# One hybrid attention layer on one core: gated-linear-attention scores and states joined, the first FoX scores begun with the third tile, and low parts put in fixed places

## The chip, the core and the metric

The kernel runs on one core of one Trainium2 chip. The metric is the device time of one execution in microseconds (us). The engines are named as in the profile: PE (TensorE, the matrix multiplier, with PEld for its weight loads), DVE (VectorE), ACT (ScalarE), POOL (GpSimd) and SP (SyncE, which issues most DMAs here). Each works through its own list of instructions in order, and waits on semaphores of the others.

## What is computed

One layer on 512 frames of width 1024 (`D`), after an RMSNorm. One wide projection feeds three branches; each is gated by a sigmoid, the sum goes through `w_out`, and an MLP with squared ReLU follows. Cut to what the change touches:

```python
# FoX branch: 8 heads of 64, causal softmax with a decay F
s = einsum('bhqd,bhkd->bhqk', q, k) * scale + F_q - F_k
p = softmax(where(k_pos <= q_pos, s, -inf)); out = p @ v
# GLA branch: 4 heads, dk 64, dv 128, chunks of 64 frames
a_causal = (q * exp(b)) @ (k * exp(-b)).T
a_anti   = (q * exp(-b)) @ (k * exp(b)).T
attn     = where(lower, a_causal, a_anti)
o = attn @ v + (q * exp(b)) @ state        # state carried from chunk to chunk, decayed
# third branch: cross attention into 256 memory tokens
merged = gate0 * y_gla + gate1 * y_fox + gate2 * y_mem
h = h + merged @ w_out;  h = h + relu(rms(h) @ w_ff1)**2 @ w_ff2
```

## The kernel before

**Numbers in two parts.** A float32 operand of a large product is split into a high part (a cast by ACT, names ending in `h` or `hi`) and a low part (source minus high part, a subtraction by DVE, names ending in `l` or `lo`). `mm3` (lines 154 to 157) then makes three matmuls of each product: high by high, low by high, high by low. Weights go through three rotating buffers: `load_w` loads one chunk, `split_w` (142) splits it; the cast is line 145, the low part line 146.

**Order of work.** PE's list stands exactly as the program is written. The other engines' lists are made by a scheduler; `tc.issue_after(x)` keeps instructions behind `x` in it. `weave` (192) runs a list of steps, and between them as many units of filler as the steps' shares ask for; a unit is one k-step of a projection, three 512-column matmuls. PSUM is cut into two pools of four banks: `mmt` (85, tiles called `mm`) and `at_` (88, tiles called `a`). A tile of a pool can be written only when the last reader of the bank's former tile is done.

**FoX.** The heads go in pairs. `fox_pair(j)` projects queries and keys; their low parts `Ql` (488) and `Kl` (492) are kept in the list `pend` and written when `low_parts()` is called. `fox_scores(j)` makes the score tiles of both heads, tile i holding 128 queries by 128(i+1) keys: tiles 0 and 1 lie in two `mmt` banks, tiles 2 and 3 in four `at_` banks (537). Then follow mask, maximum, exponential (549) and the scaling by the reciprocal sum (551). `fox_turn(h)` transposes the probabilities by PE and splits them into `PTh` (ACT) and `PTl` (DVE, 209), and then calls `low_parts`; `fox_values(h)` multiplies by V (574, 575). Ahead of the first pair's scores PE makes the V projection, whose four `mmt` banks are emptied by line 209 (`V`), and four passes of `mem_rows` (386) into an `at_` bank that ACT empties in line 387.

**GLA.** Two pairs of heads. `decays(j)` makes the decay factors (755 on PE) and the four scaled operands; `key_turn(j)` transposes keys (781); `gla_scores(j, m)` makes the causal (m=0) or mirrored (m=1) scores, a matmul over 64 rows for each head (815), and copies the wanted half into `at` with eight predicated copies (818); `states(j)` makes chunk states (794; 800 and 801 on DVE); `gla_values(j)` puts both together (826, 830); `gla_turn(h)` transposes the result (847) and multiplies it by `sg` (849). Lines 876 to 881 give the steps and shares; the filler is the projections of `gla_g` and `fox_late`.

**Gates.** `gate_group` makes the gate projections by a seven-product scheme. In its first group `lefts_2` (926) makes new left operands from `u`: `xsum[1]` gets one block subtracted (928) and one added (929), then comes the cast (930) and the low part (931). The second call makes `f2h` and `f2l`, which the matmuls of block 22 read (product 3). `take(6, ...)` adds product 6 to sums called `ct` in operations of line 957.

Of the kernel before, what the change touches and what calls it, by code (L numbers as in the profile page):

```python
# [9 lines left out]
F32 = mybir.dt.float32  # L10
# [4 lines left out]
ALU = mybir.AluOpType  # L15
AX = mybir.AxisListType

P = 128
# [4 lines left out]
NT = S // P  # L23
# [41 lines left out]
def hybrid_block(ctx, tc, chunks, wst, memT, xN, cols, gffn, gfin, wup, cst, out):  # L65
    nc = tc.nc
# [5 lines left out]
    def nm(s):  # L72
        uid[0] += 1
        return f"{s}_{uid[0]}"
# [22 lines left out]
    msk_s = cp.tile([P, 2, P], U8, name="msk_s")  # L97
# [44 lines left out]
    def split_w(raw):  # L142
        hi = wp.tile([P, 1024], F32R, tag="hi", name=nm("whi"))
        lo = wp.tile([P, 1024], F32R, tag="lo", name=nm("wlo"))
        cast = nc.scalar.copy(hi, raw)  # L145
        low_now[0] = nc.vector.tensor_tensor(lo, raw, f(hi), op=ALU.subtract).ins  # L146
        cast_now[0] = cast.ins
        next_sum(cast.ins)
        return hi, lo
# [251 lines left out]
    with pool("fox") as xp:  # L401
# [121 lines left out]
        def fox_scores(j):  # L523

            qh, ql, kh, kl = QK[j]
            stat = [[xp.tile([P, NT], F32, tag=f"{g}{e}", name=nm(g)) for g in ("mx", "rs", "ri")] for e in range(2)]
            live.update({2 * j + e: [] for e in range(2)})
            low = [mmt() for _ in range(2)]
            banks = {}
            for i in range(NT):  # L530
                n = P * (i + 1)
                w = max(n, 256)
                ps = [x[:, 256 * i:256 * i + 256] for x in low] if i < 2 else [at_()[:, :n] for _ in range(2)]
                sl = slice(i * P, (i + 1) * P)
                for p, (q, k) in enumerate(((qh, kh), (qh, kl), (ql, kh))):
                    for e, a in enumerate(half):
                        nc.tensor.matmul(ps[e], q[a, sl], k[a, :w], start=p == 0, stop=p == 2)  # L537
                banks[i] = ps
            for e in range(2):
                nFb = rows[2 * j + e]  # L540
                for i in range(NT):
                    n = P * (i + 1)
                    r = (nFb[:, 7:8, :], nFb[:, 0:2, :], nFb[:, 0:7:3, :], nFb[:, 2:6, :])[i]
                    mx, rs, ri = (x[:, i:i + 1] for x in stat[e])
                    Pt = xp.tile([P, n], F32, tag=f"Pt{i}", name=nm("Pt"), bufs=2)
                    by = [x.rearrange("p (b t) -> p b t", t=P) for x in (Pt, banks[i][e][:, :n])]
                    nc.vector.tensor_tensor_reduce(out=by[0], in0=by[1], in1=r, scale=-1.0, scalar=3e38,
                                                   op0=ALU.add, op1=ALU.min, accum_out=mx)
                    nc.scalar.activation(Pt, Pt, AF.Exp, bias=mx, scale=-1.0, accum_out=rs)
                    nc.vector.reciprocal(ri, rs)  # L550
                    nc.vector.tensor_scalar(Pt, Pt, ri, None, op0=ALU.mult)
                    live[2 * j + e].append(Pt)

        def fox_turn(h):
            Ps = live.pop(h)
# [60 lines left out]
        with tc.issue_after(cast_now[0]):  # L616
            mem_split()
        run(pair)
        low_parts()

        gvg = v_chunks(OFF["gv"], lambda t, ps: nc.scalar.copy(gv[:, t, :], ps))
        T, V_, R, A = fox_turn, fox_values, fox_rows, fox_scores
# [125 lines left out]
    with pool("gla") as lp:  # L748
# [36 lines left out]
        def states(j):  # L785


            dec, kt = gs["d", j][0], gs["k", j]
            mid = gs["s", j] = lp.tile([P, NT, P], F32, tag="mid", name=nm("mid"))
            pv = at_([P, NT, P])  # L790
            for t in range(NT - 1):
                for e in range(2):
                    h = 2 * j + e
                    nc.tensor.matmul(pv[64 * e:64 * e + 64, t, :], kt[:, t, 64 * e:64 * e + 64], gv[:, t, h * P:(h + 1) * P],
                                     start=True, stop=True)
            for t in range(NT - 1):
# [4 lines left out]
                nc.vector.tensor_scalar(mid[:, t + 1, :], x, dec[:, t:t + 1], None, op0=ALU.mult)  # L801

        def gla_scores(j, m):

            _, kn, kp, qp, qn = gs["d", j]
            kk, qq = ((kn, qp), (kp, qn))[m]
            if m == 0:
                gs["a", j] = [lp.tile([P, NT, P], F32, tag=f"at{e}", name=nm("at")) for e in range(2)]
                for at in gs["a", j]:
                    nc.gpsimd.memset(at, 0.0)  # L810
            ps = [at_([P, NT, P]) for _ in range(2)]
            for t in range(NT):
                sl = slice(t * P, (t + 1) * P)
                for e in range(2):
                    nc.tensor.matmul(ps[e][:, t, :], kk[half[e], sl], qq[half[e], sl], start=True, stop=True)  # L815
            for e in range(2):
                for t in range(NT):
                    nc.vector.copy_predicated(gs["a", j][e][:, t, :], msk_s[:, m, :], ps[e][:, t, :])

        def gla_values(j):  # L820
            mid, qp = gs["s", j], gs["d", j][3]
# [48 lines left out]
        def gate_ready(b):  # L870
# [36 lines left out]
    with pool("outp") as op_:  # L907
# [18 lines left out]
        def lefts_2(to, block):  # L926
            with tc.issue_after(low_now[0]):
                nc.vector.tensor_tensor(xsum[1], block[0], xsum[1], op=ALU.subtract)
                nc.vector.tensor_tensor(xsum[1], xsum[1], block[1], op=ALU.add)
                cast = nc.scalar.copy(to[0], xsum[1]).ins  # L930
                nc.vector.tensor_tensor(to[1], xsum[1], f(to[0]), op=ALU.subtract)
            return cast

        loaded, summed = [None], [None]

        def gate_group(gate, wo, oh, ol, i, ready=None, last=None):
# [25 lines left out]
            def product(n, w):  # L962
                wh, wl = (t.rearrange("p (a k c) -> p a k c", a=2, k=4) for t in w)
                uh, ul = GATE[n]
                ps = mmt([P, 2, 256])
                for a in range(2):
                    for k in range(4):
                        mm3(ps[:, a, :], wh[:, a, k, :], wl[:, a, k, :], uh[:, k, :], ul[:, k, :], k == 0, k == 3)
                return ps

            def take(n, ps):
                if n == 1:
                    nc.scalar.copy(c21, ps)
                if n == 2:
                    vec(c11, c21, ps)
                    tanh(c11)
                if n == 5:
                    nc.scalar.copy(c22, ps)
                if n == 6:
                    vec(c21, c21, ps, ALU.subtract)  # L980
                    vec(c22, c22, c21, ALU.subtract)
                if n == 3:
                    vec(c12, c22, ps)
                    tanh(c12)
                if n == 7:
# [48 lines left out]
            p5 = product(5, w)  # L1034
            plus(total, "22")
            if ready is not None:
                cast = lefts_2(S2, A11)
# [478 lines left out]
```

## Time and profile before

| what | us |
|---|---|
| timed runs | 823.34, 826.22, 826.74 (median 826.22) |
| the profiled execution, its own time | 823.36 |
| its span, first to last instruction | 821.6 |
| busy: PE, DVE, ACT, POOL | 809.5, 592.4, 439.1, 103.7 |
| granted PE clock | 0.998 |

A row of the timeline has the start and the duration in us, the engine, the line, the operation, what it writes and reads, shape and count; a bracket names the idle time before it and what ended it. Rows that follow each other and look alike are merged (x2). A matmul's duration reaches past the start of the next, so the distance of two starts is what a matmul costs. A float32 matmul of this program can be more than one pass in the trace, so that eight matmuls of line 815 stand as x16.

### The profile page before, as it was taken

What the parts mean: (1) busy time and instruction counts of PE and PEld (TensorE: products, weight loads), DVE (VectorE), ACT (ScalarE), POOL (GpSimd) and SP (SyncE); (2) the same over time, 40 slices, a digit from 0 to 9 for tenths busy, and PEclk for the clock granted to TensorE, in tenths of its full rate; (3) what the DMA queues carried; (4) which work ended last, traced back from release to release, by engine and by line L of the source; (5) the groups of instructions that cost most, each with busy time, mean ns of one, the idle gap of its engine ahead of it and who ended that gap; (6) DMA issues with size and microseconds to landing.
All of it is one profiled execution on the core that took longest, in us unless ns stands there. A gap on an engine that the chain in (4) does not pass through costs nothing.

```text
span 821.6 us, 12459 instructions
## 1 busy us (share of the span) xinstructions
PE 809.5 (99%) x4791; PEld 708.1 (86%) x4791; DVE 592.4 (72%) x934; ACT 439.1 (53%) x693; POOL 103.7 (13%) x125
## 2 busy tenths in 40 slices
PE   8999999999999999999999999999999999999996
PEld 6788888888888878899999889988998899889984
DVE  5846888537555677877576647897689778887896
ACT  7654656533345234434345436774577367647764
POOL 1001100101101111132231100011001100110011
PEclk9999999999999999999999999999999999999999
DMA  9534676589688884777665604978758866896644
GB/s 332 185 102 159 177 203 204 158 239 288 166 255 241 223 243 140 154 181 182 172 186 156 198 31 128 282 159 210 247 180 179 217 219 178 185 249 197 163 80 129
DMA packets 39180, 155.60 MB, mean 189 GB/s; under 512 B 4880, under 2 KB 5840, under 8 KB 37072
## 3 DMA queue, kind: packets, MB, share of 16 engines
q1 hardware_dynamic: 27712, 95.54, 33.5%
q0 software_dynamic: 9328, 54.01, 31.7%
q10 hardware_dynamic: 2080, 5.26, 2.0%
q8 instruction: 37, 0.61, 0.3%
q14 instruction: 23, 0.19, 0.1%
HBM read 152.65 MB, written 31.49 MB: 224 GB/s over the span
## 4 chain that ended last, share of the span: by engine, by line
PE 91%; DVE 4%; DMA 2%; issue 1%; ACT 1%; POOL 1%; ACTq 0%; POOLq 0%; DVEq 0%
PE mm L155 23%; PE mm L156 23%; PE mm L157 23%; PE a L156 5%; PE a L155 5%; PE a L157 5%; DMA xn<-in_xN_dram 1%; DMA memr<-in_memT_dram 1%; PE a L575 1%; PE a L537 1%; PE a L574 1%; DVE h L1176 1%; PE a L815 1%; DVE wlo L146 1%; PE mm L537 0%
## 5 line engine op out<-in xcount | busy, mean ns | idle before, releaser
L146 DVE TENSOR_TENSOR wlo<-raw,whi 128x1024 fp32r<-128x1024 f32 x68 | 88.1, 1300 | 60.0 <-ACT whi L145 59.7
L155 PE MATMUL mm<-uhi,whi 128*128 128x512 f32 (+1 forms) x352 | 126.4, 359 | 0.0
L145 ACT CAST whi<-raw 128x1024 fp32r<-128x1024 f32 x68 | 71.3, 1051 | 100.4 <-PE mm L156 59.3
L157 PE MATMUL mm<-uhi,wlo 128*128 128x512 f32 (+1 forms) x352 | 123.8, 352 | 0.0
L156 PE MATMUL mm<-ulo,whi 128*128 128x512 f32 (+1 forms) x352 | 123.6, 351 | 0.0
L1180 ACT CAST hi<-raw 128x1024 fp32r<-128x1024 f32 x65 | 68.2, 1050 | 49.5 <-PE mm L156 34.3
L1182 DVE TENSOR_TENSOR lo<-raw,hi 128x1024 fp32r<-128x1024 f32 x65 | 79.4, 1222 | 17.4 <-ACT hi L1180 17.4
L155 PEld LDWEIGHTS mm<-uhi,whi 128*128 128x128 f32 x352 | 66.7, 189 | 10.4 <-issue 1.8
L157 PEld LDWEIGHTS mm<-uhi,wlo 128*128 128x128 f32 x352 | 66.6, 189 | 9.2
L156 PEld LDWEIGHTS mm<-ulo,whi 128*128 128x128 f32 x352 | 66.7, 189 | 8.0
L1180 ACT CAST hi<-b 128x1024 fp32r<-128x1024 f32 x40 | 41.9, 1048 | 42.0 <-PE mm L157 25.5
L157 PE MATMUL mm<-u2h,lo 128*128 128x256 f32 x224 | 63.4, 283 | 0.0
L156 PE MATMUL mm<-u2l,hi 128*128 128x256 f32 x224 | 63.4, 283 | 0.0
L155 PE MATMUL mm<-u2h,hi 128*128 128x256 f32 x224 | 63.4, 283 | 0.0
L1366 POOL DMA_DIRECT2D b<-in_wst_dram x32 | 27.4, 855 | 271.3 <-DVE lo L1182 206.8
L1182 DVE TENSOR_TENSOR lo<-b,hi 128x1024 fp32r<-128x1024 f32 x40 | 48.8, 1222 | 14.1 <-ACT hi L1180 14.0
L155 PE MATMUL mm<-hi,ch 128*128 128x512 f32 x136 | 52.9, 389 | 0.0
L156 PE MATMUL mm<-lo,ch 128*128 128x512 f32 x136 | 52.9, 389 | 0.0
L157 PE MATMUL mm<-hi,cl 128*128 128x512 f32 x136 | 52.9, 389 | 0.0
L155 PE MATMUL mm<-u2sh,hi 128*128 128x256 f32 x168 | 47.5, 283 | 0.0
L156 PE MATMUL mm<-u2sl,hi 128*128 128x256 f32 x168 | 47.5, 283 | 0.0
L157 PE MATMUL mm<-u2sh,lo 128*128 128x256 f32 x168 | 47.5, 283 | 0.0
(410 smaller groups left out, 2110.3 us busy)
## 6 DMA issues: line engine op xcount, KB each, us to landing
raw<-in_wst_dram SPq DMA_DIRECT2D x114, 512.0 KB
b<-in_wst_dram POOLq DMA_DIRECT2D x32, 512.0 KB, 5.5
raw<-T SPq DMA_DIRECT2D x28, 512.0 KB
T<-in_wst_dram POOLq DMA_DIRECT2D x12, 1024.0 KB, 10.1
b<-in_wst_dram SPq DMA_DIRECT2D x16, 512.0 KB
wb<-in_wst_dram POOLq DMA_DIRECT2D x15, 512.0 KB, 5.4
wb<-in_wst_dram SPq DMA_DIRECT2D x8, 512.0 KB
T<-in_wst_dram POOLq DMA_DIRECT2D x6, 512.0 KB, 5.2
```

The lines of the kernel that those rows point to most:

```text
L145: cast = nc.scalar.copy(hi, raw)
L146: low_now[0] = nc.vector.tensor_tensor(lo, raw, f(hi), op=ALU.subtract).ins
L155: nc.tensor.matmul(ps, lh, rh, start=start, stop=False, skip_group_check=on)
L156: nc.tensor.matmul(ps, lh, rl, start=False, stop=False, skip_group_check=on)
L157: nc.tensor.matmul(ps, ll, rh, start=False, stop=stop, skip_group_check=on)
L537: nc.tensor.matmul(ps[e], q[a, sl], k[a, :w], start=p == 0, stop=p == 2)
L574: nc.tensor.matmul(po[:, q0:], vv, PTh[:, c0:c0 + w], start=n == 0, stop=False)
L575: nc.tensor.matmul(po[:, q0:], vv, PTl[:, c0:c0 + w], start=False, stop=n == 3)
L815: nc.tensor.matmul(ps[e][:, t, :], kk[half[e], sl], qq[half[e], sl], start=True, stop=True)
L1180: nc.scalar.copy(hi, raw)
L1182: nc.vector.tensor_tensor(lo, raw, f(hi), op=ALU.subtract)
L1366: nc.gpsimd.dma_start(to[i], wst[index["B", q, i, x]], accum_op=ALU.add)
```

## The change

Four things are done.

- `fox_scores` takes the tiles of the first pair in the order 2, 3, 0, 1; the other pairs keep 0, 1, 2, 3. `live` holds the probabilities by tile number for that.
- The call of `low_parts()` ahead of the first turn is gone, so that `Ql` and `Kl` of the second pair are written by the call at the end of `fox_turn(0)`.
- `gla_scores(j)` makes both halves at once and calls `states(j)`; its predicated copies take all four chunks with one repeated mask (4 copies of 512 columns for 16 of 128 in a pair); the states go to an `mmt` bank; shares are changed, and `gla_turn(0)` is followed by `gla_turn(1)` at once.
- In the first gate group `take(6)` is issued behind the low part of the second `lefts_2`, and the split of block 22 behind the addition of line 929.

```diff
 fox_scores:
-            live.update({2 * j + e: [] for e in range(2)})
+            live.update({2 * j + e: {} for e in range(2)})
...
-            for i in range(NT):
+            order = range(NT) if j else (2, 3, 0, 1)
+            for i in order:
...
-                    live[2 * j + e].append(Pt)
+                    live[2 * j + e][i] = Pt
...
         run(pair)
-        low_parts()
...
 states:
-            pv = at_([P, NT, P])
+            pv = mmt([P, NT, P])
...
-        def gla_scores(j, m):
+        def gla_scores(j):
             _, kn, kp, qp, qn = gs["d", j]
-            kk, qq = ((kn, qp), (kp, qn))[m]
...
+            for m, (kk, qq) in enumerate(((kn, qp), (kp, qn))):
+                ps = [at_([P, NT, P]) for _ in range(2)]
+                for t in range(NT):
+                    sl = slice(t * P, (t + 1) * P)
+                    for e in range(2):
+                        nc.tensor.matmul(ps[e][:, t, :], kk[half[e], sl], qq[half[e], sl], start=True, stop=True)
                 for e in range(2):
-                    nc.tensor.matmul(ps[e][:, t, :], kk[half[e], sl], qq[half[e], sl], start=True, stop=True)
-            for e in range(2):
-                for t in range(NT):
-                    nc.vector.copy_predicated(gs["a", j][e][:, t, :], msk_s[:, m, :], ps[e][:, t, :])
+                    nc.vector.copy_predicated(ats[e], msk_s[:, m:m + 1, :].to_broadcast([P, NT, P]), ps[e])
+            states(j)
...
-            (decays, (0,), 13), (key_turn, (0,), 3), (gla_scores, (0, 0), 3), (states, (0,), 3), (gla_scores, (0, 1), 4),
-            (gla_values, (0,), 5), (decays, (1,), 4), (gla_turn, (0,), 4), (gla_turn, (1,), 4), (key_turn, (1,), 3),
-            (gla_scores, (1, 0), 3), (states, (1,), 3), (u_sum, (1,), 0), (gla_scores, (1, 1), 4), (gla_values, (1,), 6),
+            (decays, (0,), 13), (key_turn, (0,), 5), (gla_scores, (0,), 8), (gla_values, (0,), 4), (decays, (1,), 5),
+            (gla_turn, (0,), 0), (gla_turn, (1,), 4), (key_turn, (1,), 5), (gla_scores, (1,), 2), (u_sum, (1,), 6), (gla_values, (1,), 6),
...
 gate_group (lefts_2 returns the cast, the addition and the low part):
-            take(6, product(6, w))
+            p6 = product(6, w)
             plus(total, "21")
-            if ready is not None:
-                cast = lefts_2(S4, A12)
+            if ready is None:
+                take(6, p6)
+            else:
+                cast, added, low = lefts_2(S4, A12)
+                with tc.issue_after(low):
+                    take(6, p6)
                 output(j)
-                p3 = product(3, split_w(block("22")))
+                raw = block("22")
+                with tc.issue_after(added):
+                    w = split_w(raw)
+                p3 = product(3, w)
```

**The first scores on PE.** The names are the score tiles (`mm_108`, `mm_109` for tiles 0 and 1 of the two heads, `a_110` to `a_113` for tiles 2 and 3). Before, the block begins so, right behind line 386:

```order
L537 MATMUL mm_108_829<-Kh_58_530,Qh_56_528 128x256
L537 MATMUL mm_109_830<-Kh_58_530,Qh_56_528 128x256
L537 MATMUL mm_108_829<-Kl_59_531,Qh_56_528 128x256
L537 MATMUL mm_109_830<-Kl_59_531,Qh_56_528 128x256
L537 MATMUL mm_108_829<-Kh_58_530,Ql_57_529 128x256
L537 MATMUL mm_109_830<-Kh_58_530,Ql_57_529 128x256
```

Now it has the tile of 384 columns first, then the one of 512, and these two banks behind them:

```order
L538 MATMUL a_110_831<-Kh_58_530,Ql_57_529 128x384
L538 MATMUL a_111_832<-Kh_58_530,Ql_57_529 128x384
L538 MATMUL a_112_839<-Kh_58_530,Qh_56_528 128x512
L538 MATMUL a_113_840<-Kh_58_530,Qh_56_528 128x512
L538 MATMUL a_112_839<-Kl_59_531,Qh_56_528 128x512
L538 MATMUL a_113_840<-Kl_59_531,Qh_56_528 128x512
L538 MATMUL a_112_839<-Kh_58_530,Ql_57_529 128x512
L538 MATMUL a_113_840<-Kh_58_530,Ql_57_529 128x512
L538 MATMUL mm_108_829<-Kh_58_530,Qh_56_528 128x256
```

`a_113` is the bank that line 386 filled and line 387 empties; its first matmul is now the eighth of the block, ahead of the two banks that wait for V.

**The second GLA pair on DVE.** `og` is the turned result of the first pair's two heads (it frees the bank that `gla_turn` wrote), `at` the score tiles. Before:

```order
L849 TENSOR_TENSOR og_459_2876<-a_458_2871,sg0_111 128x512
L146 TENSOR_TENSOR wlo_501_3102<-raw_499_3099,whi_500_3101 128x1024
L682 TENSOR_SCALAR acc4_1903<-th_466_2921,acc4_1903 128x512
L209 TENSOR_TENSOR og0_2575<-og_459_2876,og0_2575 128x512
L849 TENSOR_TENSOR og_465_2905<-a_464_2900,sg1_112 128x512
L818 COPY_PREDICATED at_473_2947<-msk_s_73,a_475_2951 128x128 x4
L818 COPY_PREDICATED at_474_2948<-msk_s_73,a_476_2952 128x128 x4
```

Now:

```order
L848 TENSOR_TENSOR og_463_2881<-a_462_2876,sg0_111 128x512
L146 TENSOR_TENSOR wlo_501_3078<-raw_499_3075,whi_500_3077 128x1024
L209 TENSOR_TENSOR og0_2575<-og_463_2881,og0_2575 128x512
L682 TENSOR_SCALAR acc4_1903<-th_468_2915,acc4_1903 128x512
L848 TENSOR_TENSOR og_465_2890<-a_464_2885,sg1_112 128x512
L816 COPY_PREDICATED at_473_2938<-msk_s_73,a_475_2942 128x512
L816 COPY_PREDICATED at_474_2939<-msk_s_73,a_476_2943 128x512
L209 TENSOR_TENSOR og1_2576<-og_465_2890,og1_2576 128x512
L816 COPY_PREDICATED at_473_2938<-msk_s_73,a_477_2954 128x512
L816 COPY_PREDICATED at_474_2939<-msk_s_73,a_478_2955 128x512
```

DVE's list hardly differs, but both halves of the scores now want banks at once: `a_475` to `a_478` are all four of the pool, and `a_478` takes over the bank of `a_464`, which the second `og` reads.

**The first gate group on DVE.** `x1` is `xsum[1]`, `wlo_547` the low part of block 22, `f2l` the low part that product 3 reads, `ct` the operations of product 6. Before:

```order
L928 TENSOR_TENSOR x1_3000<-uhi_94,x1_3000 128x1024
L146 TENSOR_TENSOR wlo_543_3383<-raw_541_3380,whi_542_3382 128x1024
L146 TENSOR_TENSOR wlo_547_3402<-raw_545_3399,whi_546_3401 128x1024
L929 TENSOR_TENSOR x1_3000<-x1_3000,ulo_95 128x1024
L957 TENSOR_TENSOR ct_523_3185<-ct_523_3185,mm_540_3348 128x2x256
L957 TENSOR_TENSOR ct_524_3186<-ct_524_3186,ct_523_3185 128x2x256
L931 TENSOR_TENSOR f2l_520_3182<-x1_3000,f2h_519_3181 128x1024
```

Now:

```order
L926 TENSOR_TENSOR x1_2985<-uhi_94,x1_2985 128x1024
L146 TENSOR_TENSOR wlo_543_3359<-raw_541_3356,whi_542_3358 128x1024
L927 TENSOR_TENSOR x1_2985<-x1_2985,ulo_95 128x1024
L146 TENSOR_TENSOR wlo_547_3378<-raw_545_3375,whi_546_3377 128x1024
L929 TENSOR_TENSOR f2l_520_3158<-x1_2985,f2h_519_3157 128x1024
L955 TENSOR_TENSOR ct_523_3161<-ct_523_3161,mm_540_3324 128x2x256
L146 TENSOR_TENSOR wlo_550_3416<-wb_521_3159,whi_549_3415 128x1024
L955 TENSOR_TENSOR ct_524_3162<-ct_524_3162,ct_523_3161 128x2x256
```

The addition stands one place earlier, and `f2l` ahead of both operations on `ct`.

More of the change, by code (lines that the diff above doesn't have):

```diff
@@ L540, in fox_scores @@
                 nFb = rows[2 * j + e]
-                for i in range(NT):
+                for i in order:
                     n = P * (i + 1)
@@ L801, in states @@
                 nc.vector.tensor_scalar(mid[:, t + 1, :], x, dec[:, t:t + 1], None, op0=ALU.mult)
-        def gla_scores(j, m):
+        def gla_scores(j):
             _, kn, kp, qp, qn = gs["d", j]
-            kk, qq = ((kn, qp), (kp, qn))[m]
[L807 to L811, printed above, removed]
-            for t in range(NT):
-                sl = slice(t * P, (t + 1) * P)
+            ats = gs["a", j] = [lp.tile([P, NT, P], F32, tag=f"at{e}", name=nm("at")) for e in range(2)]
+            for at in ats:
+                nc.gpsimd.memset(at, 0.0)
+            for m, (kk, qq) in enumerate(((kn, qp), (kp, qn))):
[4 more added lines that the diff above has]
+                        nc.tensor.matmul(ps[e][:, t, :], kk[half[e], sl], qq[half[e], sl], start=True, stop=True)
                 for e in range(2):
-                    nc.tensor.matmul(ps[e][:, t, :], kk[half[e], sl], qq[half[e], sl], start=True, stop=True)
-            for e in range(2):
-                for t in range(NT):
-                    nc.vector.copy_predicated(gs["a", j][e][:, t, :], msk_s[:, m, :], ps[e][:, t, :])
+                    nc.vector.copy_predicated(ats[e], msk_s[:, m:m + 1, :].to_broadcast([P, NT, P]), ps[e])
+            states(j)
         def gla_values(j):
@@ L928, in lefts_2 @@
                 nc.vector.tensor_tensor(xsum[1], block[0], xsum[1], op=ALU.subtract)
-                nc.vector.tensor_tensor(xsum[1], xsum[1], block[1], op=ALU.add)
+                added = nc.vector.tensor_tensor(xsum[1], xsum[1], block[1], op=ALU.add).ins
                 cast = nc.scalar.copy(to[0], xsum[1]).ins
-                nc.vector.tensor_tensor(to[1], xsum[1], f(to[0]), op=ALU.subtract)
-            return cast
+                low = nc.vector.tensor_tensor(to[1], xsum[1], f(to[0]), op=ALU.subtract).ins
+            return cast, added, low
         loaded, summed = [None], [None]
@@ L1036, in gate_group @@
             if ready is not None:
-                cast = lefts_2(S2, A11)
+                cast = lefts_2(S2, A11)[0]
                 with tc.issue_after(cast):
```

## The prediction

> **What bounds the kernel now.** I read the page first, for the engine that binds, then the waits of PE, and then the timeline of PE, DVE and ACT at the places where the order of instructions differs: 75 to 105 us (FoX), 274 to 304 us (GLA) and 340 to 349 us (first gate group).
>
> ```profile
> PE 809.5 (99%) x4791; PEld 708.1 (86%) x4791; DVE 592.4 (72%) x934; ACT 439.1 (53%) x693; POOL 103.7 (13%) x125
> ```
>
> PE has work in 99% of the span. The change neither adds nor removes a matmul, so it can gain only what PE waits, or loses where the matmul's shape changes, and it can lose only by making PE wait. The waits of PE by cause, in us in total, times, and longest:
>
> ```profile
> PE a L279 <- POOL wz L276: 1.3, 1, 1.3
> PE a L341 <- DVE xn L329: 1.0, 1, 1.0
> PE mm L156 <- DVE f2l L931: 1.0, 1, 1.0
> ...
> PE mm L537 <- DVE V L209: 0.2, 1, 0.2
> ```
>
> The first two lie at the program's start and are not touched. The third and the last are touched: gate and first scores. The other terms are too small for this list and are read from distances of starts.
>
> **First scores of FoX.** PE here, the last pass of line 386 first:
>
> ```profile
> 76.85 0.60 PE L386 MATMUL a<-gv,cst_s 128*128 128x128 f32 x4
> 77.50 0.38 PE L537 MATMUL mm<-Kh,Qh 64*128 64x256 f32 x1
> 78.10 0.38 PE L537 MATMUL mm<-Kh,Qh 64*128 64x256 f32 x1 [0.21 <-DVE V L209]
> ...
> 80.23 0.50 PE L155 MATMUL mm<-uhi,whi 128*128 128x512 f32 x1
> ```
>
> and the same block of the next pair, where nothing is waited for:
>
> ```profile
> 102.25 0.39 PE L537 MATMUL mm<-Kh,Qh 64*128 64x256 f32 x2
> 102.47 0.28 PE L537 MATMUL mm<-Kl,Qh 64*128 64x256 f32 x2
> 102.59 0.28 PE L537 MATMUL mm<-Kh,Ql 64*128 64x256 f32 x2
> ...
> 103.82 0.40 PE L537 MATMUL a<-Kl,Qh 64*128 64x512 f32 x2
> 104.05 0.40 PE L537 MATMUL a<-Kh,Ql 64*128 64x512 f32 x2
> 104.38 0.50 PE L155 MATMUL mm<-uhi,whi 128*128 128x512 f32 x1
> ```
>
> Undisturbed the block takes 104.38 − 102.25 = 2.13. Line 386 ends its four passes about .44 behind 76.85, and a change to 64 rows costs about .09 (below), so the block could start at 77.38 and end at 79.51, not 80.23: at most .72 to gain. With tile 2 first, its three pairs take about .27 + .17 + .17 and end at 77.99. Then head 1's tile of 512 columns wants the bank that line 387 on ACT empties:
>
> ```profile
> 77.79 0.38 ACT L387 COPY gv<-a 128x256 f32<-128x256 f32 x1
> ```
>
> That ends at 78.17, .06 more for the signal (in the gate, below, `f2l` ends at 348.72 and PE starts at 348.77): a new wait of .24. The `mmt` banks come last, well behind V. The block ends at 79.75, a gain of .48; I take **−.4**, bounds 0 to −.72. What hides the new order behind the scores: both heads' tile 3 are masked and exponentiated first, and the transposes of head 0 come only some 15 us later.
>
> **Values of head 0.** PE, then DVE:
>
> ```profile
> 95.12 0.39 PE L574 MATMUL a<-PTh,V 128*128 128x512 f32 x1
> 95.58 0.50 PE L575 MATMUL a<-PTl,V 128*128 128x512 f32 x1
> ```
>
> ```profile
> 91.84 0.68 DVE L488 SCALAR_TENSOR_TENSOR Ql<-mm,Qh 128x512 fp32r<-128x512 f32 x1
> ...
> 94.24 0.68 DVE L492 TENSOR_TENSOR Kl<-mm,Kh 128x512 fp32r<-128x512 f32 x1
> 94.84 1.27 DVE L209 TENSOR_TENSOR PTl<-a,PTh 128x512 fp32r<-128x512 f32 x2
> ```
>
> Line 575 comes .46 after line 574; the usual distance of 512 columns is .23 (103.82 to 104.05 above). It waits for `PTl`, which stands behind `Ql` and `Kl`. With those two (.6 each by starts) behind the turn, `PTl` is done before PE asks: **−.23**, bounds 0 to −.23. `Ql` and `Kl` then end at about 96.3 and are read from 102.25 on, the banks they free from about 100.8: covered by 4 us.
>
> **GLA, joined blocks.** One block of 16 score passes:
>
> ```profile
> 274.28 0.39 PE L157 MATMUL mm<-uhi,wlo 128*128 128x512 f32 x1
> 274.60 1.16 PE L815 MATMUL a<-qpos,kn 64*128 64x128 f32 x16
> 275.69 0.50 PE L155 MATMUL mm<-uhi,whi 128*128 128x512 f32 x1
> 276.03 0.39 PE L156 MATMUL mm<-ulo,whi 128*128 128x512 f32 x1
> ```
>
> Entering costs .32 where .23 is usual (+.09); the first pair of FoX scores costs .22 where the next ones cost .12 (+.10); the matmul after leaving costs .34 for .23 (+.11), and the last FoX pair before leaving takes .33 (104.05 to 104.38) for .23 (+.10). A visit to the 64-row shape thus costs about .40 beyond its work. Two score blocks made one save .40 a pair. The states (128 rows, 64 columns) joined on save between 0 and .40; I take half, .21, since one exit and one entry go and one change of shape stays. Two pairs: 2 × .61 = **−1.2**, bounds −.8 and −1.6.
>
> [...]
>
> The predicated copies go from 16 of 128 columns to 4 of 512 in a pair. The narrow ones are
>
> ```profile
> 275.80 1.69 DVE L818 COPY_PREDICATED at<-msk_s,a 128x128 f32<-128x128 uint8 x8 [2.96 <-PE a L815]
> ```
>
> .20 each by starts. No row shows a wide one, or a repeated mask. From below, four narrow ones less their overhead, some .5; from above there is no row with a mask, the nearest being other 512-column DVE operations at .68. I take .6 to .7, which costs nothing (rival four prices more).
>
> **A new wait at the second pair's scores.** All four `at_` banks are now asked for at once, and the last is that of `gla_turn(1)`, free when the second `og` is read. ACT and DVE there:
>
> ```profile
> 299.96 1.05 ACT L145 CAST whi<-raw 128x1024 fp32r<-128x1024 f32 x1 [4.32 <-PE mm L156]
> ```
>
> ```profile
> 301.04 1.23 DVE L146 TENSOR_TENSOR wlo<-raw,whi 128x1024 fp32r<-128x1024 f32 x1 [1.21 <-ACT whi L145]
> 302.19 0.69 DVE L682 SCALAR_TENSOR_TENSOR acc<-th,acc 128x512 f32<-128x512 f32 x1
> 302.79 0.68 DVE L209 TENSOR_TENSOR og<-og,og 128x512 fp32r<-128x512 f32 x1
> 303.50 0.69 DVE L849 TENSOR_TENSOR og<-a,sg 128x512 f32<-128x512 f32 x1
> ```
>
> From the cast's start: 1.08 to the low part, 1.15, .60, .60 and .70 to the end of the second `og`, 4.13, and .06 to PE. The cast starts .42 after a matmul of line 156. From that matmul PE has two more (.46), twelve of units (2.73), the entry (.09) and the first half's scores (.9) to do before it asks for the bank: 4.17. The bank is free at .42 + 4.13 + .06 = 4.61, so PE waits **+.44**. Bounds: 0, and +1.6 if one more low part (1.14) stands ahead. Queued behind that matmul is all of PE.
>
> **First gate group.** DVE, ACT and PE:
>
> ```profile
> 342.77 2.35 DVE L146 TENSOR_TENSOR wlo<-raw,whi 128x1024 fp32r<-128x1024 f32 x2
> 345.04 1.22 DVE L929 TENSOR_TENSOR x<-x,ulo 128x1024 f32<-128x1024 f32 x1
> 346.17 0.68 DVE L957 TENSOR_TENSOR ct<-ct,mm 128x512 f32<-128x512 f32 x1
> ...
> 347.50 1.22 DVE L931 TENSOR_TENSOR f2l<-x,f2h 128x1024 fp32r<-128x1024 f32 x1
> ```
>
> ```profile
> 346.29 1.05 ACT L930 CAST f2h<-x 128x1024 fp32r<-128x1024 f32 x1 [3.55 <-DVE x L929]
> ```
>
> ```profile
> 347.40 0.38 PE L155 MATMUL mm<-f2h,whi 128*128 128x256 f32 x1
> 348.77 0.38 PE L156 MATMUL mm<-f2l,whi 128*128 128x256 f32 x1 [0.99 <-DVE f2l L931]
> ```
>
> PE could have started line 156 at 347.52 (a matmul of 256 columns is .12) and started at 348.77: 1.25 lost. Now the addition stands one low part (1.13) earlier, at 343.9; the cast follows from 345.16 to 346.21; `f2l` takes the place of the first `ct`, runs from 346.24 and is done at about 347.4, with .06 for the signal 347.5. That is when PE asks. Gain **−1.2**, bounds −.9 (ACT late by .3) and −1.25. The low part of block 22 and the sums of product 6 that slip behind are needed by PE about a us after DVE has them.
>
> **Sum.** −.4 − .23 − 1.2 + .44 − 1.2 = **−2.6**, so the profiled execution, 823.36 with its span of 821.6, would be 820.8. With best ends everywhere −3.8; with the worst, 0 + 0 − .8 + 1.6 − .9 = −.1. The four executions of before (823.34, 823.36, 826.22, 826.74) differ by 3.4 among themselves, more than the sum; the profiled one is 2.9 below the median of the timed three. I take their mean, 824.9, as the level: **822.3**. About 0.5%, 4.1 us, is what a measurement of this kernel can tell from no change.
>
> **Rivals.**
> 1. *The waits only change place.* The bank wait at the second pair's scores is 1.6, not .44, and the first scores wait for line 387 as long as for V before. For it: DVE's list behind the cast has no gap there. Against: the sum from the cast has no free place for a further low part. Gain 1.0: 823.9. Chance .15.
> 2. *No new wait at all.* The cast comes a unit earlier, and scores to states is free: −3.6, 821.3. Chance .10.
> 3. *The gate does not do what it says.* `f2l` has a margin of only .1; if ACT starts `f2h` a us late, behind another cast of 1.05, about 1.0 of the 1.2 is lost: −1.6, 823.3. Against: ACT had been idle for 3.55 us there. Chance .04.
> 4. *Slower, by the wide predicated copies.* The mirrored copies and, behind them, the five operations of the `mid` chain (.29 each) must be done for lines 826 and 830:
>
> ```profile
> 280.31 0.29 DVE L801 TENSOR_SCALAR mid<-mid,dec 128x128 f32<-128x128 f32 x1
> ```
>
> ```profile
> 284.31 1.95 PE L826 MATMUL a<-gv,at 128*128 128x128 f32 x16
> ```
>
> Line 826 came behind 24 units and comes behind 26 now (shares 26 of 68, and of 64), less the saved .8: about 284.9. The scores come behind 18 units, not 15, and the copies begin at about 278.6. Four copies have 6.3 us, so they cost from 1.6 each on. At 2.5 each they cost 3.7 less a little in the first pair and about 2 in the second, some 5 together: +2.4, 827.3; at 2.1 the gain is cancelled. For it: no row shows a repeated mask. Against: 2.5 is three times as dear per column as the narrow copies. Chance .05.
>
> **How the numbers follow.** The forecast's own case has .66. The range goes from the best sum at the lowest level, 823.36 − 3.8 = 819.6, to the worst at the highest, 826.74 − .1 = 826.6; it holds rivals one to three and leaves out most of the fourth. The executions lie about half at the lower level and half at the higher, and a gain of 2.6 passes 4.1 only with after's runs at the lower level: faster .35, same .62, slower .03 (a loss of over 4.1 needs copies of 2.7 us and more).
>
> **What the changed profile would show.** Right: line 537 starts at about 77.4 with 384 columns and shows one wait, on line 387, of under .3; lines 574 and 575 lie .23 apart; one block of scores and states per pair, .4 to .8 shorter than its parts; a wait of about .4 on `og` in the second pair; the wait on `f2l` gone. Wrong: wide copies over 1.5 us, a wait of line 826 or 830, over a us of wait on `og`, or `f2l` still named among PE's waits.

## The result, and the profile after

| what | us |
|---|---|
| before, 8 executions | median 823.66 (823.04 to 826.74) |
| changed, 8 executions | median 820.06 (819.25 to 822.02) |
| ratio | 0.9949, 95% interval 0.9934 to 0.9965 |
| changed, measured a second time | median 819.81, ratio 0.9957, interval 0.9945 to 0.9968 |
| the profiled execution of the changed kernel, its own time | 822.02 (span 820.2) |

The change is faster by about 0.5%, both intervals lie wholly under no change, and in both measurements the slowest execution of the changed kernel (822.02 and 822.46) is faster than the fastest of before (823.04 and 822.8). The waits of PE in the changed kernel, by the same view as before (us in total, times, longest):

```profile
PE a L279 <- POOL wz L276: 1.3, 1, 1.3
PE a L341 <- DVE xn L329: 1.2, 1, 1.2
PE mm L157 <- DVE lo L268: 0.8, 1, 0.8
PE a L156 <- DVE lo L268: 0.3, 1, 0.3
```

The waits on `f2l` and on `V` are no longer in the list; what is left lies at the program's start. Yet the two profiled executions differ by only 1.4 in span (821.6 to 820.2). The reason lies ahead of every changed instruction: between 24 and 28 us the clock granted to PE was .57 in the profiled execution of the changed kernel. The windows view has the stretch, its length, then the busy times of PE, PEld, DVE, ACT and POOL with counts, the clock, the DMA share and GB/s; before first, then the changed kernel:

```profile
24.00:28.00 4.00, 4.00 (x24) 3.37 (x23) 3.72 (x5) 3.36 (x5) 0.00 (x0) 1.00 0.24 72
```

```profile
24.00:28.00 4.00, 4.00 (x12) 3.04 (x12) 3.37 (x4) 1.92 (x3) 0.00 (x0) 0.57 0.21 58
```

Twelve matmuls got through in place of 24. PE came out of it 1.86 late: .23 it had brought along from earlier waits, and 1.6 were lost here. So the spans are no measure of the change here, and I use another one: both kernels issue 4791 matmuls, and where the order agrees, the n-th of one is the n-th of the other. The difference of their two starts is how far PE is ahead or behind at that place, and what a place gains is the step of that difference across it. The steps are good to about .03.

| step across | predicted | changed, first profile | changed, second profile |
|---|---|---|---|
| first FoX scores | −.4 | −.42 | −.40 |
| values of head 0 | −.23 | −.54 | −.54 |
| GLA, with its new wait | −1.2 + .44 = −.76 | −.99 | −.99 |
| gate | −1.2 | −1.23 | −1.22 |
| sum | −2.6 | −3.2 | −3.15 |

PE at the first scores of the changed kernel; all times here are 1.86 later than before's for the reason given:

```profile
78.71 0.60 PE L386 MATMUL a<-gv,cst_s 128*128 128x128 f32 x4
79.24 0.45 PE L538 MATMUL a<-Kh,Qh 64*128 64x384 f32 x2
...
79.87 0.71 PE L538 MATMUL a<-Kh,Qh 64*128 64x512 f32 x2
80.10 0.70 PE L538 MATMUL a<-Kl,Qh 64*128 64x512 f32 x2
80.42 0.60 PE L538 MATMUL a<-Kh,Ql 64*128 64x512 f32 x2
...
81.67 0.50 PE L155 MATMUL mm<-uhi,whi 128*128 128x512 f32 x1
```

The block begins .53 behind line 386, as worked out, and takes 81.67 − 79.24 = 2.43, which is .30 over the undisturbed 2.13. This fits the new wait for the bank of line 387, which is on ACT from 79.65 to 80.03; the list of waits does not name it.

PE at the second GLA pair, and the wide copies of the first pair on DVE:

```profile
303.31 1.16 PE L814 MATMUL a<-qpos,kn 64*128 64x128 f32 x16
304.31 1.47 PE L814 MATMUL a<-qneg,kp 64*128 64x128 f32 x16
305.70 0.88 PE L794 MATMUL mm<-gv,kt 128*64 128x128 f32 x12
```

```profile
279.45 2.58 DVE L816 COPY_PREDICATED at<-msk_s,a 128x512 f32<-128x512 uint8 x4
```

The mirrored half takes 1.39 from start to the states, the causal half 1.00: the .4 of the bank wait. A wide copy is .62 from start to start, where four narrow ones took .8.

The gate, PE and DVE:

```profile
347.17 0.28 PE L155 MATMUL mm<-f2h,whi 128*128 128x256 f32 x1
347.44 0.39 PE L156 MATMUL mm<-f2l,whi 128*128 128x256 f32 x1
347.67 0.28 PE L157 MATMUL mm<-f2h,wlo 128*128 128x256 f32 x1
```

```profile
343.82 1.22 DVE L927 TENSOR_TENSOR x<-x,ulo 128x1024 f32<-128x1024 f32 x1
344.96 1.22 DVE L146 TENSOR_TENSOR wlo<-raw,whi 128x1024 fp32r<-128x1024 f32 x1
346.16 1.23 DVE L929 TENSOR_TENSOR f2l<-x,f2h 128x1024 fp32r<-128x1024 f32 x1
```

`f2l` ends at 347.39; PE starts on it at 347.44, .27 behind the matmul before (.12 is usual). What was 1.37 is now .27, a gain of 1.10. The other .13 of the step lies one matmul ahead: before, line 155 came .36 behind its predecessor, just after the cast of `f2h` had ended (346.29 + 1.05 = 347.34), and now it comes .23 behind.

### The profile page after: what moved, and what is told of

The parts are those of the page before. It is cut to its first block, busy times and chain, and to the rows that moved or that the text cites. A ratio compares the mean times of both kernels' runs of the same rounds, so it can differ in the third digit from the quotient of the medians.

```text
span 820.2 us, 12435 instructions
## 1 busy us (share of the span) xinstructions
PE 809.4 (99%) x4791; PEld 710.2 (87%) x4791; DVE 591.4 (72%) x910; ACT 439.1 (54%) x693; POOL 103.7 (13%) x125
## 4 chain that ended last, share of the span: by engine, by line
PE 94%; DVE 2%; DMA 2%; issue 1%; ACT 0%; POOL 0%; ACTq 0%; POOLq 0%; DVEq 0%
PE mm L155 24%; PE mm L156 23%; PE mm L157 23%; PE a L156 5%; PE a L157 5%; PE a L155 5%; DMA xn<-in_xN_dram 1%; DMA memr<-in_memT_dram 1%; PE a L538 1%; PE a L576 1%; PE a L575 1%; DVE h L1181 1%; PE a L814 1%; DVE lo L1187 0%; PE a L825 0%
```

## The experiments

My theory was that each place is a wait (or a change of shape) of its own on an engine that is busy 99% of the time, so that what it gains stays gained, and that the values of head 0 had been undersized. The rival was that gains are handed on: the next wait takes them back. The steps of all runs, measured as above (a run's own start of up to 2.8 late or .7 early is taken out by this):

| run | first scores | values | GLA | gate |
|---|---|---|---|---|
| scores only | −.40 | −.26 | 0 | 0 |
| low parts only | +.66 | −.52 | 0 | 0 |
| gate, sums only | +.70 | +.06 | 0 | −.11 |
| gate, split only | 0 | +.04 | 0 | −.73 |
| GLA only | +.05 | +.05 | −.44 | +.02 |
| GLA only, again | 0 | 0 | −1.02 | +.01 |
| V first (on before) | −.67 | +.67 | 0 | 0 |
| states apart (on changed) | −.41 | −.53 | −.49 | −1.24 |
| copies three times (on changed) | −.40 | −.53 | +2.71 | −1.23 |
| two og buffers (on changed) | −.40 | −.50 | −1.41 | −1.25 |
| og and V first (on changed) | −.66 | −.48 | −1.41 | −1.23 |

**The order of the first scores alone**, on the kernel before.

```diff
+            order = range(NT) if j else (2, 3, 0, 1)
-            for i in range(NT):
+            for i in order:
```

> The kernel before with the new order of the first FoX scores alone. Measured by the start of the same PE matmul here and in the kernel before. Theory one (waits are local, what is saved stays saved): .42 earlier behind the first scores, as in the changed kernel, and still .42 earlier behind the values of head 0. Rival (the next wait takes it back): .42 earlier behind the scores, but with Ql and Kl still ahead of PTl on DVE the values of head 0 wait that much longer, and nothing is left behind them.

Measured: −.40 at the scores and another −.26 at the values. Theory one has the first number; neither had the second. DVE of this run first, then one row of DVE in the kernel before:

```profile
92.25 1.22 DVE L146 TENSOR_TENSOR wlo<-raw,whi 128x1024 fp32r<-128x1024 f32 x1
93.38 0.69 DVE L492 TENSOR_TENSOR Kl<-mm,Kh 128x512 fp32r<-128x512 f32 x1
93.98 1.28 DVE L209 TENSOR_TENSOR PTl<-a,PTh 128x512 fp32r<-128x512 f32 x2
```

```profile
87.34 0.17 DVE L550 RECIPROCAL ri<-rs 128x1 f32<-128x1 f32 x1 [0.54 <-ACT Pt L549]
```

`PTl` starts at 93.98 for 94.84. Before, DVE stood .54 for an exponential; with the wide tiles' exponentials first it does not, and the scheduler has put `Ql` 3 us further ahead.

**The low parts alone**, on the kernel before.

```diff
         run(pair)
-        low_parts()
```

> The kernel before with only the call of the low parts moved behind the turn. By the changed kernel's trace the values of head 0 gained .54 (four PE starts, .23 + .11 + .10 + .10), where the prediction had .23. Theory one: the low parts alone bring all of it, .54, since every PTl of the head came late and not only the first. Rival: .23 from the low parts, and the rest came from the new order of the scores (its third tile is ready earlier).

Measured: −.52 at the values, so the low parts alone bring all of it, as theory one has it. PE of the kernel before shows where I had not looked: behind the rows that the prediction quotes, lines 574 and 575 go on with late starts. The single row after them is ACT's last cast of `PTh` for this head.

```profile
95.91 0.34 PE L574 MATMUL a<-PTh,V 128*128 128x384 f32 x1
96.17 0.44 PE L575 MATMUL a<-PTl,V 128*128 128x384 f32 x1
96.45 0.28 PE L574 MATMUL a<-PTh,V 128*128 128x256 f32 x1
96.57 0.32 PE L575 MATMUL a<-PTl,V 128*128 128x256 f32 x1
96.73 0.28 PE L574 MATMUL a<-PTh,V 128*128 128x256 f32 x1
```

```profile
92.99 0.39 ACT L208 CAST PTh<-mm 128x256 fp32r<-128x256 f32 x1
```

and the changed kernel:

```profile
96.77 0.39 PE L576 MATMUL a<-PTl,V 128*128 128x512 f32 x1
97.00 0.33 PE L575 MATMUL a<-PTh,V 128*128 128x384 f32 x1
97.17 0.34 PE L576 MATMUL a<-PTl,V 128*128 128x384 f32 x1
```

From 95.58 on the distances are .33, .26, .28, .12, .16; in the changed kernel they are .23, .17, .17, .12, .12. The first wait is the .23 that I counted, and .10, .09, .11, 0 and .04 follow it, .57 in all. They are not all waits for `PTl`. The .09 is one: the second `PTl` ends at about 96.11 on DVE, and line 575 starts on it at 96.17. The .10 and .11 stand ahead of matmuls of line 574, which read `PTh`, done since 93.38: the matmul that has waited is itself dearer, by about .10 to the next start. The two halves of the gain are not a sum either: the new order alone brings −.26 here, the low parts alone −.52, both together −.54.

The same run shows +.66 at the first scores, which this kernel does not change, and the next run +.70. DVE of that next run (gate, sums only):

```profile
75.85 0.76 DVE L521 TENSOR_TENSOR nFb<-nFb,cst_s 128x128 f32<-128x128 f32 x2 [0.61 <-DMA nFb<-dF]
76.53 0.74 DVE L394 SCALAR_TENSOR_TENSOR mvl<-gqT,gv,mvh 128x512 fp32r<-128x512 f32 x1
77.19 1.28 DVE L209 TENSOR_TENSOR V<-mm,V 128x512 fp32r<-128x512 f32 x2
```

DVE stood .61 for a DMA, and `V` is queued behind it. PE's list of waits has 1.0 on `V` there, for 0.2 in the profile of before. So the wait that the new order avoids is not one size: of six executions with the old order and the old queue, four lost .6 and two about 1.3, and those two are the ones in which DVE stood for that DMA (.57 and .61).

**The sums of product 6 alone, and the split of block 22 alone**, each on the kernel before.

```diff
-            take(6, product(6, w))
+            p6 = product(6, w)
...
+                cast, added, low = lefts_2(S4, A12)
+                with tc.issue_after(low):
+                    take(6, p6)
```

```diff
-                p3 = product(3, split_w(block("22")))
+                raw = block("22")
+                with tc.issue_after(added):
+                    w = split_w(raw)
+                p3 = product(3, w)
```

> The kernel before with only the sums of product 6 put behind f2l in the first gate group. The cast f2h still ends at about 347.3, so f2l moves from 347.5 to about 347.4: PE's wait on f2l shrinks by .1 to .2, of the 1.23 that both halves of the edit brought. Rival: the two operations on ct were the whole delay, and .6 or more is gained.

> The kernel before with only the split of block 22 put behind the addition. f2h then ends at about 346.2, but one operation on ct stands ahead of f2l still: f2l starts at about 346.8, and the gain is about .6 to .75. With the other half alone (.1 to .2) that makes less than the 1.23 of both: neither half alone is enough. Rival: f2l stays where it was (347.5) since DVE has as much ahead of it as before, gain 0.

Measured −.11 and −.73, as expected; together −.84, not −1.23. With the sums alone `f2l` has the way free, but its source is late:

```profile
345.53 1.22 DVE L929 TENSOR_TENSOR x<-x,ulo 128x1024 f32<-128x1024 f32 x1
347.86 1.22 DVE L931 TENSOR_TENSOR f2l<-x,f2h 128x1024 fp32r<-128x1024 f32 x1 [1.12 <-ACT f2h L930]
```

With the split alone the source is early, and one of the sums stands ahead:

```profile
343.30 1.22 DVE L929 TENSOR_TENSOR x<-x,ulo 128x1024 f32<-128x1024 f32 x1
344.44 1.22 DVE L146 TENSOR_TENSOR wlo<-raw,whi 128x1024 fp32r<-128x1024 f32 x1
345.57 0.68 DVE L957 TENSOR_TENSOR ct<-ct,mm 128x512 f32<-128x512 f32 x1
346.17 1.22 DVE L931 TENSOR_TENSOR f2l<-x,f2h 128x1024 fp32r<-128x1024 f32 x1
```

Two things held `f2l`, its source and its place in the queue, and each alone hides what the other would bring.

**The states as a step of their own**, on the changed kernel.

```diff
-            states(j)
...
-            (gla_scores, (0,), 8)
+            (gla_scores, (0,), 4), (states, (0,), 4)
-            (gla_scores, (1,), 2), (u_sum, (1,), 6)
+            (gla_scores, (1,), 2), (u_sum, (1,), 2), (states, (1,), 4)
```

> The changed kernel with the states as a step of their own again, four units behind the joined scores. In the changed kernel both pairs together gained .98 on PE. Theory one (a change of the matmul's shape costs, but one visit less costs less): the first pair loses about .2 of its .64, the second likewise, so that PE stands about .4 to .5 later behind GLA than in the changed kernel. Rival A (the step from scores to states drains as much as a visit): no difference, 0. Rival B (it is free): .8 later.

Measured: GLA gains .49 for .99. Joining the states on is worth .25 a pair: between the rivals, next to the half that was forecast. Without its visit of its own the block of states saves the entry (.09) and the dear matmul after leaving (.11), .20 of the .25, and the change from scores to states still costs: .20 from the last score to the first state in the changed kernel (279.32 to 279.53, and 305.50 to 305.70 in the second pair), where .11 is a pair's distance. Two changes of shape next to each other thus cost .25 less here than two with units between them.

**Each wide copy three times**, on the changed kernel.

```diff
+                    for _ in range(3):
-                    nc.vector.copy_predicated(...)
+                        nc.vector.copy_predicated(...)
```

> The changed kernel with each wide predicated copy made three times (the same data, the same result). A copy is .62 from start to start, so 5.0 more per pair on DVE. Theory one (the copies have about 6.3 in the first pair before they cost): the twelve take 7.4, and line 825 or 829 on PE waits about 1.0 in the first pair and about as much in the second. Rival: the copies are off the path, 0. Other rival: the low part of the weights behind them on DVE comes late, and PE waits for that, 3 or more.

Measured: GLA goes from −.99 to +2.71, so 3.7 is lost. PE's waits name it:

```profile
PE a L826 <- DVE at L817: 3.0, 3, 1.6
```

In the first pair PE loses 1.2 at line 826 (1.0 expected); in the second 1.8 and then .4, twice as much as expected. Its copies do not have less time, 7.6 from their start (306.37) to PE's readiness for line 826 (313.98) for 6.5 in the first pair, but DVE has other work among them, a low part of the weights above all:

```profile
313.16 0.74 DVE L817 COPY_PREDICATED at<-msk_s,a 128x512 f32<-128x512 uint8 x1
313.78 1.23 DVE L146 TENSOR_TENSOR wlo<-raw,whi 128x1024 fp32r<-128x1024 f32 x1
314.90 0.73 DVE L817 COPY_PREDICATED at<-msk_s,a 128x512 f32<-128x512 uint8 x1
```

The mechanism of the fourth rival is real, with the threshold that it gave for the first pair; at .62 a copy, the four need 2.5 of the 6.5.

**Two buffers for og**, on the changed kernel.

```diff
-            og = lp.tile([P, S], F32, tag="og", name=nm("og"))
+            og = lp.tile([P, S], F32, tag="og", name=nm("og"), bufs=2)
```

(and the same for `tt`, which shares the tag).

> The changed kernel with two buffers for og in place of one, so that the second og needs not wait until DVE has made the low part of the first (behind the weights' low part). Theory one: the .42 that PE lost in the second pair's mirrored scores came from the bank that the second og reads; it is gone, and PE stands .4 earlier behind GLA than in the changed kernel. Rival: the cast of og, now ahead of the cast of the weights on ACT, makes the weights late, and a wait on wlo takes the place, 0 or worse.

Measured: GLA gains 1.41 for .99, and the mirrored half takes as long as the causal one:

```profile
304.29 1.16 PE L814 MATMUL a<-qpos,kn 64*128 64x128 f32 x16
305.29 1.06 PE L814 MATMUL a<-qneg,kp 64*128 64x128 f32 x16
306.28 0.88 PE L794 MATMUL mm<-gv,kt 128*64 128x128 f32 x12
```

So the wait that the change added came from one buffer: the second `og` could not be written before DVE had made the low part of the first, and that stood behind the low part of the weights. (The run gives `tt` a second buffer too, and no run parts the two; it is `og` that reads the bank.)

**V ahead of nFb**, on the kernel before.

```diff
-                    nc.vector.tensor_tensor(nFb[:, b, :], nFb[:, b, :], m, op=ALU.add)
+                    with tc.issue_after(v_low[-1]):
+                        nc.vector.tensor_tensor(nFb[:, b, :], nFb[:, b, :], m, op=ALU.add)
```

(`v_low` keeps the instructions of line 209 that `v_evac` makes).

> The kernel before, with the order of the scores unchanged, but the four additions to nFb (which wait for a DMA) put behind the V evacuations on DVE. In other runs of the same code PE lost .6 or 1.3 at the first scores, and where it lost 1.3 DVE had stood .6 for that DMA. Theory one: V waits only for what stands ahead of it on DVE; the block of scores takes its undisturbed 2.13, .72 earlier than in the kernel before, in any run. Rival: V itself is late by PE or ACT, and less than .2 is gained.

Measured: −.67 at the first scores, as expected, and +.67 at the values of head 0. PE there:

```profile
94.04 0.39 PE L576 MATMUL a<-PTh,V 128*128 128x512 f32 x1
95.16 0.50 PE L577 MATMUL a<-PTl,V 128*128 128x512 f32 x1 [0.74 <-DVE PTl L209]
```

This is the rival that gains are handed on, in full: with `Ql` and `Kl` ahead of `PTl`, DVE sets when the values can go on, and all that PE had won is waited away. A gain at the first scores thus reaches the end only where `PTl` comes earlier as well. The new order does that by itself (scores only kept its −.40 with the low parts where they were, since `Ql` moved ahead); the old order needs the low parts behind the turn (og and V first, below).

**og and V first together, and the changed kernel again**, both on the changed kernel and timed side by side; the first also takes the tiles of the first pair in the old order.

> The changed kernel with two buffers for og, the additions to nFb behind the V evacuations, and the first pair's scores in the old order 0, 1, 2, 3 (V comes in time then, and tile 3 comes behind line 387). Theory one: .43 from og as measured, and the first scores take 2.13 for 2.43, another .3, if PTl, now without Ql and Kl ahead of it, keeps up (the wait that took back the gain with the old low parts was about 1.2, and Ql and Kl take 1.2): about .7 under the changed kernel, ratio to before .9945 to .9955. Rival: PTl does not keep up without the new order of the exponentials, and the values of head 0 give back .3 to .7: no gain over the changed kernel but og's .43.

> The changed kernel once more, in rounds beside the kernel above. The traces give −3.2 where the DMA of nFb is in time, and about .7 more in executions where it is not: a ratio of .995 to .996. Rival: the medians of the timed runs (−3.6, ratio .9949) hold something that the traces do not show, and the ratio is under .994 or over .998 here.

Measured: 819.29 (ratio .9948, interval .9935 to .9961) and 819.81 (ratio .9957, .9945 to .9968). By the steps the first is ahead by .26 at the scores and .42 in GLA and behind by .06 at the values, .6 in all, and the medians differ by .5; the intervals overlap, so the timed runs alone do not tell the two apart. The changed kernel's second ratio agrees with the traces' −3.2 (.996 of 823.65). That it is up to .7 more where the DMA is late is not shown: in no trace with the new order did DVE stand for that DMA.

**GLA alone**, twice, on the kernel before (the diff of `states`, `gla_scores` and the shares as in the change).

> The kernel before with the GLA part of the change alone. Theory one (the parts add up, each has its own place on PE): PE stands .98 earlier behind GLA (.64 in the first pair, .22 in the second, .1 from the two turns in one), and nothing is given back or won at the gate, where the wait on f2l stays. Rival: the earlier arrival at the gate makes PE wait longer for f2l, so that up to .9 of it is lost.

> The GLA part alone once more. In the run before, the second pair's bank wait was .9 and not .42, because a weight transfer of POOL's queue took 11.6 from issue to landing (8.2 to 9.2 in the other traces), and the memset of ex behind the next one on POOL came 2.0 late for DVE. Theory one (that is a matter of the one execution): the transfer takes 8 to 9.5, DVE does not wait for ex by more than .3, the bank wait is about .4 and the gain behind GLA about .98. Rival (it belongs to this kernel, whose PE reaches GLA at another time than the changed kernel's): the transfer takes over 11 again, and the gain is about .45 as before.

Measured: −.44 and then −1.02. In the first of the two the bank wait was .9 and not .4. PE, then DVE, then POOL:

```profile
304.74 1.16 PE L814 MATMUL a<-qneg,kp 64*128 64x128 f32 x14 [0.38 <-DVE og L848]
```

```profile
298.26 0.69 DVE L769 TENSOR_TENSOR kn<-gkT,ex 128x512 f32<-128x512 f32 x1 [2.01 <-POOL ex L766]
```

```profile
297.51 0.58 POOL L132 DMA_DIRECT2D T<-T  x1 [4.22 <-DMA T<-in_wst_dram]
```

A weight transfer on POOL took 11.6 to land, the next issue waited for it, the small memset `ex` stood behind that issue, and DVE with `og` behind the memset. In the second run it took 9.1, and the gain was the changed kernel's. DVE's wait for `ex` was .71 there, more than the .3 expected, and PE did not feel it. The gate's wait was the same in both (1.0 in PE's list), so nothing was handed on to it.

## Why the prediction was right and where it failed

The step that failed is the last one, from the sum to what a measurement can tell. The prediction held that "About 0.5%, 4.1 us, is what a measurement of this kernel can tell from no change", and gave the outcome "same" .62. What the runs showed in its place: the medians of eight executions each are 3.6 apart, 0.51%, with an interval of about ±0.16%. Even the 2.6 of the sum, 0.32% of 823.66, would have stood clear of that. In the sum itself the term most off was the values of head 0, −.54 for −.23.

- **What binds** was right: in the traces all steps lie at PE's waits and changes of shape in the places that were named.
- **First scores**: right, −.42 for −.4, with the new wait on line 387 (.30 for .24). Not seen was that the wait taken away varies from one execution to the next, .6 or 1.3, by a DMA ahead of `V` on DVE.
- **Values of head 0**: the mechanism was right and the size off. The step said "**−.23**, bounds 0 to −.23"; it measured −.54. It counted the length of the first wait alone. Left at nothing were the second late `PTl` (.09) and the dearer matmul behind each wait (.10 and .11). The distances of four more rows would have shown it.
- **Joined blocks**: −.64 in the first pair for −.61, and the bounds held. About .1 came beside it, between the pairs, where the two turns now follow each other; that was not priced.
- **The new wait**: right, +.42 for +.44, and shown to come from the one buffer of `og`, which the prediction took for an order of DVE's queue. The rival of 1.6 did not come about; .9 did, once.
- **The gate**: right, −1.23 for −1.2, and it needed both halves of the edit.
- **The level** failed: "I take their mean, 824.9, as the level". The median of before turned out at 823.66; two of its eight executions lie near 826, and none of eleven in the second measurement. What sets that upper level was not traced in the kernel before; the two runs here of 826.3 (low parts only, copies three times) both had the slow stretch of the clock described below (.63 and .57 between 24 and 28 us). Of the 2.2 that the forecast of 822.3 lies over 820.06, 1.2 is the level, .6 the sum's size, and .4 is not accounted for by the traces.
- **The chances** failed with the last step: the 4.1 was not worked out from any run, and beside it stood the 3.4 by which four single executions differ. That is the spread of executions; the interval of a median of eight is narrower. The second measurement gave −0.43%, with ±0.12%, and is clear of no change as well.
- **Rival two**, which did not come about, was added up wrongly: −2.6 without the wait of .44 and with .19 more for each pair's states makes −3.4, not −3.6.

## What to carry to other kernels

Where an engine is busy 99% of the time, price a wait by the whole row of late starts behind it, the dearer matmul after each wait (about .10 here) included, and not by the first alone, and look for the second wait that stands ready to take a gain back. When an instruction is late, ask for its source, its place in the queue and its buffer one by one: mending one of them can bring almost nothing while the others hold (.11 of the gate's 1.23 here). Before two profiled executions are subtracted, find out where their difference begins, here ahead of anything that was changed. And take what can be told from no change out of the interval of the medians, not out of the spread of single executions.

## What the runs showed of the hardware

- The granted clock fell to .57 to .63 between 24 and 28 us in 5 of the 14 traces (changed kernel, copies three times and the second run of GLA alone .57, two og buffers .61, low parts only .63), whatever the kernel, and in those PE reached the first FoX scores 1.9 to 2.8 later than in the profile of before. 1.6 of that was lost in the stretch itself: from line 156 behind its wait on `lo` to the next row of line 341 PE took 4.22 in the changed kernel's profile, 4.21 in low parts only and 4.22 in copies three times, for 2.63 in the profile of before.
- In the changed kernel's profile the recorded clock is .50 from 24.02 to 27.44 and 1.00 on either side, and 512-column matmuls start .43 apart and not .23, from 24.12 to 27.11. The stretch comes behind a wait of PE on `xn` of 1.2; another trace (states apart) has the same wait and a clock of 1.00, so that wait alone does not decide it. What does is not shown. (The first run of GLA alone has a low clock at another place: .83 between 3 and 12 us and .98 between 12 and 20.)
- Three waits read here cost PE more than their length: the matmul that had waited took about .10 more (before, 95.58 to 95.91 is .33 for .23 and 96.17 to 96.45 is .28 for .17; after, 347.44 to 347.67 is .23 for .12).
- One weight transfer of POOL's queue took 8.2 to 9.2 from issue to landing in 13 traces (9.0 in the profile of before, 8.3 in the changed kernel's) and 11.6 in one, the first run of GLA alone, and what stood behind it on POOL was 2.0 late for DVE.
